# Adding half of the expert outputs on the chip instead of in DRAM, in a two-block layer on one core

## The chip, the cores and the metric

The kernel runs on one core of one Trainium2 chip. The metric is the device time of one execution in microseconds; lower is better. Times of runs are given as a median with the lowest and the highest.

## The reference, cut to what matters

Two transformer blocks run one after the other on 512 tokens of width 1024, in float32. Only the end of the second block matters here: a mixture of 32 experts in four groups, of which every token takes two.

```python
def hierarchical_moe(h, w_rg, b_rg, w_re, b_re, w_gate, w_up, w_down):
    ...
    out = jnp.zeros_like(tok)
    for e in range(N_EXPERTS):
        hid = jax.nn.silu(tok @ w_gate[e]) * (tok @ w_up[e])
        out = out + combine[:, e:e + 1] * (hid @ w_down[e])
    return out.reshape(b, s, d)
...
        x = x + gate_f * hierarchical_moe(h, ...)
    return rmsnorm(x, norm_final)
```

`w_gate[e]` and `w_up[e]` are 1024 x 256, `w_down[e]` is 256 x 1024; one expert has 3 MB of weights. `combine` is zero but for the two experts of each token.

## The kernel before, in words

Everything ahead of the experts (first block, mixer, router) is not touched. Then 17 *units* follow (`units`, line 1176): 16 pairs of experts and one unit "x" of 64 slots for the tokens that did not fit into a pair. A pair has 128 slots, 64 for each expert; a slot holds a token's number (`slot_t`, `slot_i`) and its weight (`slot_w`). In the loop's order the units have the places 0 to 16, "x" is place 4.

For a unit the loop at line 1771 does this:

- `load_piece` (line 1183) loads the expert weights in pieces of 1 MB, in SP's queue, into a ring of places in SBUF (`ring`, line 1607): a piece goes where the piece 17 places earlier was. The halves of a unit's gate and up weights come first, then its down weights.
- `gather` (line 1581, POOL's queue, an indirect DMA) fetches the 128 tokens of the unit two places later from `hs` in DRAM.
- `gate_up` (line 1634) is 16 matmuls in float32 (32 in the profile, since each float32 matmul has two entries there), two experts side by side on 64 columns each; ScalarE and VectorE make `hid`.
- `front` (line 1614) transposes the gathered tokens of the next unit into `xe`.
- `hid_T` (line 1646) transposes `hid` into `hT_`.
- `down` (line 1654) multiplies by the down weights, 8 matmuls (16 entries) into two banks; VectorE scales both halves into `y`.
- `scatter_add` (line 1589, POOL's queue, an indirect DMA with addition) adds the rows of `y` to the tokens' rows in `yd`, a tensor in DRAM that holds the residual stream.

The last unit (place 16) is not added in DRAM. In the loop's `else` the 512 rows of `yd` are read back into `xtok` in four DMAs of 512 KB on SP's queue (line 1797), which wait for all 16 additions, and `combine` (line 1675) adds the last unit on the chip: `down` builds a one-hot table `oh` of 128 x 512 (slot against token), a matmul with `oh` as the stationary operand brings the slots' rows to their tokens, and VectorE adds the bank to `xtok`. Eight blocks (four token tiles, two column halves) make one call. `finish_half` then normalises and stores.

`down` and `combine` know two forms already: with `yl` given, `y` is split into a rounded part `yh` and a rest `yl`, both in the rounded format F32R, and both are multiplied; without it `y` stays float32. The form with two parts was used only in the loop behind the end for tokens beyond "x", which does not run here.

The order on each engine is planned when the program is built: instructions that are ready in the planner's model may come ahead of earlier ones of the program text; each engine then runs its list in order. A small set of tile names is shared: `whi` and `wlo` (three buffers each) hold weight pieces as well as the tiles `parts_y` and `ylast` take.

Of the kernel before, what the change touches and what calls it, by code (L numbers as in the profile page):

```python
# [19 lines left out]
F32 = mybir.dt.float32  # L20
F32R = mybir.dt.float32r
# [24 lines left out]
def tile_kernel(ctx: ExitStack, tc: tile.TileContext, A, out, dbg=None, stop=None):  # L46
    nc = tc.nc
# [11 lines left out]
    def mm(ps, l, r, start, stop):  # L59
        nc.tensor.matmul(ps, l, r, start=start, stop=stop, skip_group_check=True)  # L60

    def bk():
        return ps_mm.tile([128, 512], F32, name="mm")
# [171 lines left out]
    with tc.tile_pool(name="b1x", bufs=1, reuse_waits="tile") as b1x:  # L235
# [14 lines left out]
        for k in range(8):  # L250
# [10 lines left out]
            if k >= 3 and k < 7:  # L261
                i = k - 3
# [285 lines left out]
    with tc.tile_pool(name="mgs", bufs=1, reuse_waits="tile") as mgs, \  # L548
            tc.tile_pool(name="mg", bufs=1, reuse_waits="tile") as mg:
        mrg = (mg.tile([128, 8, 512], F32R, name="mrh"), mg.tile([128, 8, 512], F32R, name="mrl"))  # L550
        for m in range(8):
            sg = []
            for i in range(2):
                c0 = 3072 + i * 1024 + m * 128
                ps = dense(wload(w_in[:, c0:c0 + 128], 8, 128), u)
                t = mgs.tile([128, 512], F32, name="sg", bufs=6)
# [150 lines left out]
    with ExitStack() as mls:  # L707
# [25 lines left out]
        for hf in range(2):  # L733
            hid = (ml.tile([128, 16, 512], F32R, name="hidh"), ml.tile([128, 16, 512], F32R, name="hidl"))
            for m in range(16):
                c0 = hf * 2048 + m * 128
                ps = dense(wload(A["w_mlp_in"][0][:, c0:c0 + 128], 8, 128), u)
                t = ml.tile([128, 512], F32, name="rl", bufs=3)
# [5 lines left out]
            for m in range(8 - hf):  # L744
# [5 lines left out]
                t = ml.tile([128, 512], F32, name="mo", bufs=2)  # L750
# [12 lines left out]
        t = ml.tile([128, 512], F32, name="mo", bufs=2)  # L763
# [41 lines left out]
    for ts in halves:  # L805
        for k in range(8):
            t = n2.tile([128, 256], F32, name="hmt", bufs=6)
# [349 lines left out]
    xtok = me.tile([128, 4, 1024], F32, name="xtok")  # L1157
# [18 lines left out]
    units = list(range(XU)) + ["x"] + list(range(XU, NP))  # L1176
# [6 lines left out]
    def load_piece(n, place, e=None, eng=None, cols=False):  # L1183

        u, a, i = todo[n]
        pick = lambda w: w[NP * i + u] if e is None else w[bass.ds(e, 1)].rearrange("a k n -> (a k) n")
        if cols:
            for j, t in enumerate(place):
                nc.sync.dma_start(t.rearrange("p (k n) -> p k n", k=2),
                                  pick(wd_)[:, j * 512:(j + 1) * 512].rearrange("(p k) n -> p k n", p=128))  # L1190
            places[n] = None, place
            return


        ws = (pick(wd_),) if a == 2 else (pick(wg_), pick(wu_))
        kb = (2 if a == 2 else 4) // len(place)
        for j, t in enumerate(place):
            k0 = (0 if a == 2 else 4 * a) + j * kb
            for g, w in enumerate(ws):
                (eng or nc.sync).dma_start(t.rearrange("p (g k n) -> p g k n", k=kb, g=len(ws))[:, g],  # L1200
                                           w.rearrange("(p k) n -> p k n", p=128)[:, k0:k0 + kb, :])
        places[n] = place

    def weights(u):

        def block(ns, k, w):
            kb = 2048 // w
            place = places[ns[k // kb]]
            if place[0] is None:
                return [t[:, k * 512:(k + 1) * 512] for t in place[1]]  # L1210
            k, kb = k % kb, kb // len(place)
            if w == 512:
                return place[k // kb].rearrange("p (g k n) -> p k g n", g=2, k=kb)[:, k % kb]
            b = place[k // kb][:, k % kb * w:(k % kb + 1) * w]
            return [b[:, :512], b[:, 512:]]
        ns = [[todo.index((u, a, i)) for a in range(3)] for i in ((0,) if u == "x" else (0, 1))]
        return [(lambda k, n=n: block(n[:2], k, 512), lambda k, n=n: block(n[2:], k, 1024)) for n in ns]
# [135 lines left out]
    yd = dr.tile([512, 1024], F32, name="yd")  # L1353
# [227 lines left out]
    def gather(idx):  # L1581
        x = wp.tile([128, 1024], F32, name="raw", bufs=NRAW)
        n = idx.shape[0]
        gathers.append(nc.gpsimd.indirect_dma_start(out=x[:n], out_offset=None, in_=hs,
                                     in_offset=bass.IndirectOffsetOnAxis(ap=idx, axis=0),
                                     bounds_check=511, oob_is_err=False))
        return x
# [9 lines left out]
    mw = ctx.enter_context(tc.tile_pool(name="mw", bufs=1, side="right", reuse_waits="tile"))  # L1597
# [36 lines left out]
    def gate_up(xe, ws, n):  # L1634

        pg = ps_s.tile([128, 512], F32, name="sc")
        for k in range(8):
            for h, w in enumerate(ws):
                pq = slice(64 * h, 64 * h + 64)
                mm(pg[pq].rearrange("p (g n) -> p g n", g=2), xe[:, k, pq], w[0](k), k == 0, k == 7)  # L1640
        hid = mw.tile([128, 256], F32, name="hid")
        silu[0] = nc.scalar.activation(hid[:n], pg[:n, :256], AF.Silu)  # L1642
        nc.vector.tensor_mul(hid[:n], hid[:n], pg[:n, 256:])
        return hid
# [9 lines left out]
    def down(hT_, ws, n, tokf, wsl, yh, yl=None):  # L1654

        oh = None
        if tokf is not None:
            oh = mw.tile([128, 512], F32R if yl is not None else F32, name="oh", bufs=1)
            nc.vector.tensor_scalar(oh[:n], io512[:n], tokf, None, op0=OP.is_equal)
        for j in range(2):  # L1660
            c = slice(j * 512, (j + 1) * 512)
            py = bk()
            for k in range(2):
                for h, w in enumerate(ws):
                    pq = slice(64 * h, 64 * h + 64)
                    mm(py[pq], hT_[:, k, pq], w[1](k)[j], k == 0, k == 1)
            y = yh[:, c] if yl is None else sqacc
            nc.vector.scalar_tensor_tensor(y[:n], py[:n], wsl, gfb[:n, c], op0=OP.mult, op1=OP.mult)
            if yl is None:
                continue  # L1670
            nc.scalar.activation(yh[:n, c], y[:n], AF.Copy)
            nc.vector.tensor_sub(yl[:n, c], y[:n], yh[:n, c].bitcast(F32))
        return n, oh, yh, yl

    def combine(parts, done=None):

        for i, j in [(m % 4, m // 4) if done is None else (m // 2, m % 2) for m in range(8)]:
            c = slice(j * 512, (j + 1) * 512)
            ps = bk()
            ms = [(oh[:n, i * 128:(i + 1) * 128], y[:n, c]) for n, oh, *ys in parts for y in ys if y is not None]  # L1680
            for k, (t, y) in enumerate(ms):
                mm(ps, t, y, k == 0, k == len(ms) - 1)
            nc.vector.tensor_add(xtok[:, i, c], xtok[:, i, c], ps)
            if done:
                done(i, j)
# [68 lines left out]
    def over_slots():  # L1754

        lp = ps_t.tile([64, NX], F32, name="tp")
        for n in range(8):
            mm(lp, POt[:, n, :], CT[:, n, 0, :], n == 0, n == 7)
        lw = ps_t.tile([64, 3, NX], F32, name="tp")
        for n in range(8):  # L1760
            mm(lw, POw[:, n, :], CW[:, n], n == 0, n == 7)
        ls = rt.tile([64, 2, NX], F32, name="ls")
        nc.vector.tensor_scalar(ls[:, 0], lp, 512.0, None, op0=OP.add)
        nc.vector.tensor_reduce(ls[:, 1], lw.rearrange("p m c -> p c m"), axis=AX.X, op=OP.add)
        nc.sync.dma_start(ltd, ls.rearrange("p a c -> p (a c)"))
        nc.vector.tensor_copy(xslot, ls[:, :, 0])
        nc.vector.tensor_copy(xslot_i, ls[:, 0, 0:1])

    parts_y = lambda: (wp.tile([128, 1024], F32R, name="whi", bufs=NHI), wp.tile([128, 1024], F32R, name="wlo", bufs=NLO))
    ylast = lambda: wp.tile([128, 1024], F32, name="whi", bufs=NHI)  # L1770
    for t, u in enumerate(units):
        n, tokf, wsl, idx = slot(u)
        e = nc.sync.value_load(eid[0:1, 0:1], min_val=0, max_val=NE - 1) if u == "x" else None
        for m, key in enumerate(todo):
            if key[0] == u and m not in places:
                place = ring[m - 2]
                if m == len(todo) - 1 and len(place) == 1:

                    place = [place[0][:, :1024], place[0][:, 1024:]]
                load_piece(m, place, e, cols=m == len(todo) - 1)  # L1780
        ws = weights(u)
        if t + 2 < len(units):
            xs_[units[t + 2]] = gather(slot(units[t + 2])[3])
        hid = gate_up(xe_[u], ws, n)
        if t == 0:
            over_slots()
        if t + 1 < len(units):
            v = units[t + 1]
            xe_[v] = front(xs_[v], slot(v)[0])
        hT_ = hid_T(hid, n)  # L1790
        if t + 1 < len(units):
            y = mw.tile([128, 1024], F32, name="y", bufs=2)
            down(hT_, ws, n, None, wsl, y)
            scatter_add(idx, y[:n])
        else:
            for i in range(4):
                nc.sync.dma_start(xtok[:, i, :], yd[i * 128:(i + 1) * 128, :])
            parts = [down(hT_, ws, n, tokf, wsl, ylast())]


    nf = wp.tile([128, 1024], F32, name="raw", bufs=NRAW)
# [24 lines left out]
    with tc.For_i(0, more, 1) as it:  # L1826
# [11 lines left out]
        ws = weights("x")  # L1838
# [37 lines left out]
```

## Time and profile before

| | before |
|---|---|
| median of 3 runs | 1392.52 us (1388.49 to 1395.84) |
| profiled execution, its own time | 1396.43 us |
| span of that execution | 1394.6 us |
| granted TensorE clock, mean share | 0.971 |
| busy share of the span: PE, DVE, ACT, POOL | 92%, 50%, 33%, 14% |
| stage of the experts | about 1090 to 1370 us |

PE is TensorE's matmuls, DVE VectorE, ACT ScalarE, POOL GpSimd, SP the engine whose queue loads the weights. The span lies inside the run's own time. Durations of matmuls overlap in the records; their pitch is read from start to start. In the rows, "idle before" is the time that the engine stood still in front of an instruction, and the name behind the arrow is what ended it. `L60` is the helper that records nearly all matmuls; they are told apart by their tiles: `sc` is gate-up, `mm<-...,hT_` the down matmuls, `mm<-...,oh` the additions by one-hot table, `tp<-ident,raw` and `po` the transposes. The number behind `hT__` names the unit: 9490 is place 0, 9909 place 6, 10135 place 9, 10634 place 16.

### The profile page before, as it was taken

Reading aid. Unit: us, or ns where it says so; the run is one execution under the profiler, and the core shown is the slowest. Engines: PE = TensorE matmul, PEld = TensorE weight load, DVE = VectorE, ACT = ScalarE, POOL = GpSimd, SP = SyncE. Lnnn points to the kernel's source line nnn. Section 1 sums busy time; section 2 is a strip of 40 time slices with the busy share of each in tenths; the row PEclk is TensorE's granted clock in tenths of the full one; section 3 lists DMA queues with packets and bytes.
Section 4 is the critical chain, followed back from the end, with each engine's and each line's share of the span. In section 5 each row is a group of like instructions: output and inputs, shape, how many; then the busy total and the mean of one; then the engine's idle time right before and its main releaser. Section 6 shows DMA issues by size and latency. Waiting matters only on the chain.

```text
span 1394.6 us, 20149 instructions
## 1 busy us (share of the span) xinstructions
PE 1287.2 (92%) x8021; PEld 946.3 (68%) x8021; DVE 700.8 (50%) x1187; ACT 458.7 (33%) x803; POOL 194.4 (14%) x227
## 2 busy tenths in 40 slices
PE   7999999999989999999999989999999599877874
PEld 6797778888878788887888876986667244322321
DVE  6546677534477764347457543256674522212214
ACT  4343343423444322334235514424535111101103
POOL 2000002000312200132112000001031121211101
PEclk9899999999999999999999999999999699999998
DMA  7222225335357754336341522231775799999994
GB/s 220 73 80 70 76 58 162 117 91 156 91 181 255 234 178 145 95 96 207 93 134 53 152 58 69 85 84 54 256 263 181 268 386 356 367 365 319 400 363 152
DMA packets 202351, 245.56 MB, mean 176 GB/s; under 512 B 11733, under 2 KB 161199, under 8 KB 198416
## 3 DMA queue, kind: packets, MB, share of 16 engines
q1 hardware_dynamic: 194848, 226.49, 49.0%
q0 software_dynamic: 7392, 17.76, 4.4%
q8 instruction: 64, 1.05, 0.3%
q14 instruction: 31, 0.25, 0.1%
q10 hardware_dynamic: 16, 0.00, 0.0%
HBM read 232.15 MB, written 19.19 MB: 180 GB/s over the span
## 4 chain that ended last, share of the span: by engine, by line
PE 68%; DMA 18%; DVE 7%; issue 3%; ACT 3%; SPq 0%; POOL 0%; DVEq 0%; ACTq 0%; POOLq 0%
PE mm L60 53%; PE sc L60 10%; DMA adw<-in_w_ada_dram 3%; PE po L60 3%; DMA ON<-in_expert_w_up_dram 2%; DMA pc<-in_expert_w_up_dram 2%; PE tp L60 1%; DMA pc<-in_expert_w_gate_dram 1%; DVE adacc L609 1%; DVE wlo L115 1%; DMA ON<-in_expert_w_down_dram 1%; DMA ON<-in_expert_w_gate_dram 1%; DMA pc<-in_expert_w_down_dram 1%; DMA mh<-in_expert_w_down_dram 1%; DMA mh<-in_expert_w_up_dram 1%
## 5 line engine op out<-in xcount | busy, mean ns | idle before, releaser
L114 ACT ACTIVATE whi<-raw 128x1024 fp32r<-128x1024 f32 (+1 forms) x157 | 163.4, 1043 | 367.7 <-PE mm L60 276.6
L115 DVE TENSOR_TENSOR wlo<-raw,whi 128x1024 fp32r<-128x1024 f32 (+1 forms) x157 | 195.6, 1248 | 173.1 <-ACT whi L114 172.9
L60 PE MATMUL mm<-uh,whi 128*128 128x512 f32 x528 | 210.6, 399 | 2.9 <-ACT uh L154 1.5
L60 PE MATMUL mm<-ul,whi 128*128 128x512 f32 x528 | 209.9, 398 | 0.5 <-DVE ul L155 0.5
L60 PE MATMUL mm<-uh,wlo 128*128 128x512 f32 x528 | 209.5, 397 | 0.0
L60 PE MATMUL sc<-pc,xe 128*64 128x512 f32 x296 | 106.5, 623 | 14.0 <-DMA pc<-in_expert_w_up_dram 13.7
L60 PEld LDWEIGHTS mm<-uh,whi 128*128 128x128 f32 x528 | 100.8, 191 | 26.2 <-ACT uh L154 2.3
L60 PEld LDWEIGHTS mm<-ul,whi 128*128 128x128 f32 x528 | 100.8, 191 | 23.6 <-issue 1.7
L60 PEld LDWEIGHTS mm<-uh,wlo 128*128 128x128 f32 x528 | 101.0, 191 | 22.2 <-issue 1.0
L60 PE MATMUL mm<-hidh,whi 128*128 128x512 f32 (+1 forms) x272 | 103.9, 382 | 0.0
L60 PE MATMUL mm<-hidh,wlo 128*128 128x512 f32 (+1 forms) x272 | 103.2, 379 | 0.0
L60 PE MATMUL mm<-hidl,whi 128*128 128x512 f32 (+1 forms) x272 | 102.0, 375 | 0.0
L740 POOL TENSOR_TENSOR rl<-rl 128x512 f32<-128x512 f32 x32 | 50.2, 1568 | 228.6 <-ACT rl L739 228.6
L1642 ACT ACTIVATE hid<-sc 128x256 f32<-128x256 f32 (+1 forms) x17 | 6.5, 383 | 210.6 <-PE sc L60 210.6
L60 PEld LDWEIGHTS sc<-pc,xe 128*64 128x64 f32 x296 | 33.1, 143 | 58.6 <-issue 55.2
L609 DVE SCALAR_TENSOR_TENSOR adacc<-adw,cact,adacc 128x1024 f32<-128x1024 f32 x42 | 56.9, 1356 | 25.5 <-DMA adw<-in_w_ada_dram 24.8
L60 PE MATMUL mm<-mh,whi 128*128 128x512 f32 (+1 forms) x168 | 67.9, 404 | 0.0
L60 PE MATMUL mm<-mh,wlo 128*128 128x512 f32 (+1 forms) x168 | 66.8, 398 | 0.0
L60 PE MATMUL mm<-mlo,whi 128*128 128x512 f32 (+1 forms) x168 | 66.2, 394 | 0.0
L1628 DVE TENSOR_SCALAR xe<-tp,sge 128x128 f32<-128x128 f32 (+1 forms) x68 | 24.2, 400 | 80.7 <-PE sc L60 65.1
L60 PEld LDWEIGHTS mm<-hidh,wlo 128*128 128x128 f32 x272 | 51.0, 188 | 10.6
L60 PEld LDWEIGHTS mm<-hidl,whi 128*128 128x128 f32 x272 | 51.1, 188 | 10.4 <-issue 0.2
(622 smaller groups left out, 2374.2 us busy)
## 6 DMA issues: line engine op xcount, KB each, us to landing
raw<-in_w_in_dram SPq DMA_DIRECT2D x68, 512.0 KB
adw<-in_w_ada_dram SPq DMA_DIRECT2D x24, 1024.0 KB
pc<-in_expert_w_gate_dram SPq DMA_DIRECT2D x37, 512.0 KB
pc<-in_expert_w_up_dram SPq DMA_DIRECT2D x37, 512.0 KB
raw<-in_w_mlp_in_dram SPq DMA_DIRECT2D x32, 512.0 KB
raw<-in_w_mlp_out_dram SPq DMA_DIRECT2D x32, 512.0 KB
pc<-in_expert_w_down_dram SPq DMA_DIRECT2D x16, 1024.0 KB
ON<-in_expert_w_down_dram SPq DMA_DIRECT2D x5, 1024.0 KB
```

Source lines behind the costliest of these rows:

```text
L60: nc.tensor.matmul(ps, l, r, start=start, stop=stop, skip_group_check=True)
L114: nc.scalar.activation(hi, raw, AF.Copy)
L115: nc.vector.tensor_sub(lo, raw, hi.bitcast(F32))
L609: nc.vector.scalar_tensor_tensor(acc[s], w[:, k, :], c, acc[s], op0=OP.mult, op1=OP.add)
L740: nc.gpsimd.tensor_mul(t, t, t)
L1628: nc.vector.tensor_scalar(xe[:, f, :], tp[:, k * n:(k + 1) * n], sge[:, 1, f:f + 1], sge[:, 0, f:f + 1], op0=OP.mult, op1=OP.add)
L1642: silu[0] = nc.scalar.activation(hid[:n], pg[:n, :256], AF.Silu)
```

## The change

Places 0 to 7 are still added in DRAM. At place 8 the tokens' rows are read back, now on POOL's queue, and from there on every unit's output is kept on the chip in the form with two parts; each time two units are there, the next pass of the loop adds them to `xtok` by one call of `combine` with both (four matmuls for a block instead of one). The last unit alone is added behind the loop as before, in float32. Two sets of buffers alternate: one from `whi` and `wlo`, one in the tiles that the DRAM additions used (`yh`, `yl`, in place of the two buffers of `y`). `oh` has two buffers.

```diff
--- before.py
+++ after.py
@@ -1655,7 +1655,7 @@
         oh = None
         if tokf is not None:
-            oh = mw.tile([128, 512], F32R if yl is not None else F32, name="oh", bufs=1)
+            oh = mw.tile([128, 512], F32R if yl is not None else F32, name="oh", bufs=2)
             nc.vector.tensor_scalar(oh[:n], io512[:n], tokf, None, op0=OP.is_equal)
@@ -1768,6 +1768,9 @@
     ylast = lambda: wp.tile([128, 1024], F32, name="whi", bufs=NHI)
+
+    AWAY = 8
+    ybuf, parts = [], []
     for t, u in enumerate(units):
@@ -1788,14 +1791,19 @@
         hT_ = hid_T(hid, n)
-        if t + 1 < len(units):
-            y = mw.tile([128, 1024], F32, name="y", bufs=2)
+        if t < AWAY:
+            y = mw.tile([128, 1024], F32, name="yl" if t % 2 else "yh")
             down(hT_, ws, n, None, wsl, y)
             scatter_add(idx, y[:n])
-        else:
+            continue
+        if t == AWAY:
             for i in range(4):
-                nc.sync.dma_start(xtok[:, i, :], yd[i * 128:(i + 1) * 128, :])
-            parts = [down(hT_, ws, n, tokf, wsl, ylast())]
+                nc.gpsimd.dma_start(xtok[:, i, :], yd[i * 128:(i + 1) * 128, :])
+            ybuf += [parts_y(), (mw.tile([128, 1024], F32R, name="yh"), mw.tile([128, 1024], F32R, name="yl"))]
+        if len(parts) == 2:
+            combine(parts)
+            parts = []
+        parts.append(down(hT_, ws, n, tokf, wsl, *(ybuf[t % 2] if t + 1 < len(units) else [ylast()])))
```

## Rows read from the trace of the kernel before

**Rows 1.** Busy time by stretch: us, PE, PEld, DVE, ACT, POOL, clock, DMA, GB/s.

```profile
1175.70:1187.90 12.20, 12.20 (x61) 6.40 (x60) 3.54 (x8) 1.89 (x5) 2.61 (x2) 1.00 1.03 370
1224.00:1361.00 137.00, 105.73 (x413) 37.96 (x413) 24.70 (x53) 11.05 (x31) 17.39 (x13) 0.95 0.98 363
```

**Rows 2.** PE's timeline: the first down matmul of place 0 and of place 6.

```profile
1114.64 0.60 PE L60 MATMUL mm<-pc,hT__9490 128*64 128x512 f32 x2
...
1187.22 0.64 PE L60 MATMUL mm<-pc,hT__9909 128*64 128x512 f32 x1
```

**Rows 3.** PE's timeline, places 9 to 16: matmuls that waited for weights.

```profile
1239.68 3.22 PE L60 MATMUL mm<-pc,hT__10135 128*64 128x512 f32 x11 [1.37 <-DMA pc<-in_expert_w_down_dram]
...
1242.73 0.59 PE L60 MATMUL mm<-pc,hT__10135 128*64 128x512 f32 x1
...
1253.03 1.51 PE L60 MATMUL sc<-pc,xe 128*64 128x512 f32 x6 [3.23 <-DMA pc<-in_expert_w_up_dram]
...
1269.17 0.64 PE L60 MATMUL sc<-mlo,xe 128*64 128x512 f32 x1 [1.34 <-DMA mlo<-in_expert_w_up_dram]
...
1290.55 1.09 PE L60 MATMUL sc<-pc,xe 128*64 128x512 f32 x1 [4.11 <-DMA pc<-in_expert_w_up_dram]
...
1325.56 0.61 PE L60 MATMUL sc<-mh,xe 128*64 128x512 f32 x1 [1.98 <-DMA mh<-in_expert_w_up_dram]
...
1343.78 5.30 PE L60 MATMUL sc<-pc,xe 128*64 128x512 f32 x14 [2.49 <-DMA pc<-in_expert_w_up_dram]
...
1360.87 0.61 PE L60 MATMUL sc<-ON,xe 128*64 128x512 f32 x1 [1.46 <-DMA ON<-in_expert_w_up_dram]
```

**Rows 4.** The chain that ended last, its end: start, us, what.

```profile
1336.28 14.23 DMA pc<-in_expert_w_down_dram
...
1350.57 10.16 DMA ON<-in_expert_w_up_dram
...
1360.87 3.63 PE sc L60 x14
...
1366.44 7.87 PE mm L60 x24
```

**Rows 5.** POOL's timeline: additions in DRAM (`yd<-y`) and one gather.

```profile
1211.01 1.58 POOL L1590 DMA_INDIRECT yd<-y,slot_i  x1 [11.80 <-DVE y L1668]
...
1224.33 1.61 POOL L1590 DMA_INDIRECT yd<-y,slot_i  x1 [4.43 <-DVE y L1668]
1226.24 1.03 POOL L1584 DMA_INDIRECT raw<-hs,slot_i  x1 [0.30 <-issue]
...
1355.80 1.56 POOL L1590 DMA_INDIRECT yd<-y,slot_i  x1 [16.62 <-DVE y L1668]
```

**Rows 6.** DMA queue (packets, MB, share of 16 engines), 1350 to 1360 us.

```profile
q1 hardware_dynamic: 1094, 4.11, 102.4%
```

**Rows 7.** DMA queues, 1320 to 1330 us: weights, and one addition.

```profile
q1 hardware_dynamic: 929, 3.45, 85.4%
q0 software_dynamic: 144, 0.31, 15.7%
```

**Rows 8.** DMA queues, 1338 to 1348 us: weights, and one addition.

```profile
q1 hardware_dynamic: 644, 3.38, 87.9%
q0 software_dynamic: 144, 0.25, 13.1%
```

**Rows 9.** SP's queue: its wait (us in total, times, longest), and the issues.

```profile
SPq L1797 <- DMA yd<-y,slot_i: 10.0, 1, 10.0
...
1365.70 1.77 SPq L1797 DMA_DIRECT2D xtok<-yd  x4
```

**Rows 10.** VectorE: groups and first addition; the one-hot table; TensorE's last part.

```profile
L1683 DVE TENSOR_TENSOR xtok<-xtok,mm 128x512 f32<-128x512 f32 x8 | 5.4, 681 | 0.6 <-PE mm L60 0.5
...
1371.71 0.69 DVE L1683 TENSOR_TENSOR xtok<-xtok,mm 128x512 f32<-128x512 f32 x1 [0.30 <-PE mm L60]
...
L1659 DVE TENSOR_SCALAR oh<-rbc,slot_t x1: 481/481/481, 1090.3 to 1090.3; 128x512 f32<-128x512 f32 x1
...
1370.54 7.19 PE L60 MATMUL mm<-whi,oh 128*128 128x512 f32 x16
```

**Rows 11.** POOL's timeline: another plain load of 512 KB.

```profile
1303.91 0.60 POOL L1802 DMA_DIRECT2D raw<-in_norm_final_dram  x1 [18.71 <-PE tp L1621]
```

**Rows 12.** PE's timeline in a dense stage: first and last of 54 matmuls.

```profile
699.69 0.39 PE L60 MATMUL mm<-hidh,wlo 128*128 128x512 f32 x1
...
711.82 0.39 PE L60 MATMUL mm<-hidl,whi 128*128 128x512 f32 x1
```

**Rows 13.** ScalarE, groups of the whole span: a rounding of 128 x 512.

```profile
L154 ACT ACTIVATE mrh<-t 128x512 fp32r<-128x512 f32 x8 | 5.0, 630 | 19.8 <-POOL t L569 19.8
```

## The prediction

> **What bounds the kernel now.** I read the page's slices first, then the stage of the experts alone, and in it the engines in order: TensorE's timeline, its waits, the DMA queues by stretch, the chain that ended last. Places 0 to 16 are the 17 units in the loop's order; the place with the extra experts is 4.
>
> Two regimes follow each other. In places 0 to 6 TensorE never stops (12.20 us busy of 12.20) and the weights loaded ahead are used up; from 1224 to 1361 it is busy for 105.7 of 137.0 us while the 16 DMA engines are busy for 98% [rows 1]. In the first regime six places take 1187.22 - 1114.64 = 72.6 us, so a place costs TensorE **12.1 us** when nothing is late [rows 2]. In the second, almost every place stops for its weights: the places 9, 10, 11, 12, 14, 15 and 16 each have a matmul that waited for a landing [rows 3]. The chain that ended last says the same: DMA 14.2 us, DMA 10.2 us, then place 16's gate-up, its down matmuls, and the additions [rows 4]. The last weights that count land at 1360.87; place 16's down matmuls end at 1370.54, 9.7 us later [rows 3, 10], and the output is stored by 1394.6. So what the change is worth is decided by when place 16 ends; the 24.1 us behind that are the same work in both kernels.
>
> **What it removes.** Eight additions in DRAM, of places 8 to 15, the first issued at 1224.33 and the last at 1355.80 [rows 5]. Their POOL time (1.6 us each) lies on an engine with nothing else to do. Their DMA time does not: in the ten microseconds with no addition in flight the weights' queue moved 4.11 MB [rows 6]; in two stretches with one addition in each it moved 3.45 and 3.38 MB, although the addition itself is only 0.31 and 0.25 MB [rows 7, 8]. The queue's total hardly differs, so one addition displaces 0.66 to 0.73 MB of weights, at 0.411 MB/us **1.6 to 1.8 us**. A lower bound is its bytes alone, 0.25 / 0.411 = 0.6 us. I take 1.6, since two stretches show it. The seven of places 8 to 14 have landed before 1360.9: 7 x 1.6 = 11.2 us of landing time.
>
> It also takes four read-backs out of SP's queue at the end. SP waits there 10.0 us for the last addition to land and issues them at 1365.70 [rows 9]. Behind them on SP are only the output's stores, which wait for later work, and the first addition to the tokens on VectorE started at 1371.71, 0.3 us after idling for TensorE and not for the rows [rows 10]. That removal is worth nothing by itself, but it would have become the limit had place 16 ended some microseconds sooner.
>
> **What it moves.** The same 2.1 MB are read back at place 8, by POOL. The price is 2.1 / 0.411 = **5.1 us** of landing time for whatever is in flight [rows 6], between about 1221 and 1231. Four issues at 0.60 us (the row of another plain load on POOL) are 2.4 us of POOL [rows 11]. They must wait until place 7's addition, issued at 1211.01, has landed, some 10 us later (the last addition, issued at 1355.80, was waited for until 1365.70 [rows 5, 9]). Behind them on POOL stands the gather of place 11, at 1226.24 [rows 5]; it is needed some 25 us later, so the wait is covered. If that cover went, place 11's transposes would be late.
>
> **What it adds.** Four pairs are added on the chip inside the loop, at places 10, 12, 14 and 16: each 8 blocks x 4 matmuls of 512 columns in the rounded float format. Their duration reads 0.39 us, but they overlap: in the dense stage 54 such matmuls start between 699.69 and 711.82, one every 12.13 / 53 = 0.229 us [rows 12]. So a pair costs TensorE 32 x 0.229 = **7.3 us**, four 29.3 us. An upper bound is the full duration, 0.39 x 32 = 12.5 us. I take 0.229: same shape, type and engine, each with its own weight load. The last unit alone stays as it is.
>
> VectorE gets 32 adds of 0.68 us, 16 subtractions at about that price and eight one-hot tables of 0.48 us, some 37 us [rows 10]; ScalarE 16 roundings at 0.63 us, 10 us [rows 13]. VectorE is busy for 24.7 of these 137 us and ScalarE for 11.1 [rows 1]. A block's add (0.68) is shorter than its four matmuls (0.92) and three banks rotate, so TensorE doesn't wait. The halves of one unit share one scratch tile, a serial chain of some 4 us (two adds or subtractions and a rounding, twice) behind the down matmuls; nothing needs it before the pair is added, over a place later. All this costs nothing as long as VectorE stays under half busy.
>
> The Trainium skill's page "DMA: Bandwidth & Descriptors", in "Anatomy of one DMA — SWDGE (gpsimd) path", gives a DMA of this queue a fixed 2 us, mostly waiting for the write's receipt, and movement by bytes / 436 GB/s; by that an addition of 0.25 MB takes 0.57 us of the engines, and the eight removed give back less than the read-back costs. Rows 7 and 8 speak against it for additions; by the page the sum would come out on the slow side, which is rival 2 below.
>
> **The sum.** A place whose second half of gate-up starts at landing L ends at L + 9.7 if its additions are out of the way; otherwise it ends 12.1 (with a pair 19.4) after the place before. Landings shift by +5.1 for the read-back and -1.6 for each addition that is gone.
> - Place 9 waited for 1239.68 and ended at 1243.3 [rows 3]; now +5.1 - 1.6: 1246.8.
> - 10: landing 1253.0 + 5.1 - 3.2 = 1254.9, so 1264.6; by TensorE 1246.8 + 19.4 = 1266.2. 11: landing 1269.5, 1279.2; by TensorE 1278.3.
> - 12: TensorE 1279.2 + 19.4 = 1298.6, landing 1289.3 + 9.7 = 1299.0. 13: 1311.1. 14: 1330.5 (landing 1321.1, not a limit).
> - 15: landing 1343.8 + 5.1 - 11.2 = 1337.7, so 1347.4. 16: TensorE 1347.4 + 19.4 = 1366.8; landing 1360.9 - 6.1 = 1354.8, 1364.5, or **1371.8** if the pair is added wholly behind that landing.
>
> Place 16 so ends between 1366.8 and 1371.8 against 1370.5: -3.7 to +1.3 us. The program's order is planned ahead: the one-hot table written at the end of the loop was computed at 1090.3 [rows 10], so additions that are ready probably fill the waits; but the planner's waits are not the chip's. I take -2. Against the profiled execution's own 1396.43 us that is 1394.4; the runs' median is 3.9 us lower, so 1392.52 - 2 = **1390.5**. What the DMA queues get back, TensorE's additions take.
>
> **The rivals.**
> 1. *All of the additions fall into waits.* TensorE then runs without a stop from place 9: 1246.8 + 7 x 12.1 + 29.3 = 1360.8, 9.7 us sooner: about 1383. For it: 31 us idle of 137 [rows 1], as much as the additions need. Against it: places 11, 12 and 15 still hang on landings in the sum; these would have to come some 4 us earlier again, as they would if an addition's uneven load on the engines costs more than the 1.6 us.
> 2. *The last pair stands behind the last weights, and the DMA gives nothing back.* The place is 16: with 0.6 us for each addition, seven give 4.3 us and the read-back takes 5.1, so the landing comes at 1361.7; half a gate-up and the transposes, then 7.3 us of additions before the down matmuls: 1361.7 + 9.7 + 7.3 - 0.5 = 1378.2, +7.7: about 1400. It decides as soon as an addition gives back under 0.75 us and the planner puts the pair behind the gate-up. Against it rows 7 and 8; for it that units and additions stand in that order in the program.
> 3. *The matmuls cost their duration.* 128 x 0.39 = 50 us, 20 us more than above, with TensorE the bound: about 1411. Rows 12 speak plainly against it.
>
> That the change doesn't do what it says has no case: no wait remains that could keep the eight in DRAM.
>
> **The numbers.** Forecast 0.57, its own range 1386 to 1398; rival 1 0.22, rival 2 0.16, rival 3 0.05. Range 1382.5 to 1400: it reaches to rivals 1 and 2 and leaves out rival 3 and what lies beyond them. 0.5% (7.0 us) is about what a measurement here can tell from no change. Faster by more is rival 1, 0.22; slower by more rivals 2 and 3, 0.21; within it 0.57.
>
> **What would show it.** Right: 128 matmuls of the one-hot tiles at 0.23 us from start to start; TensorE at over 90% from 1250 to 1366 and its waits for weights there down from 31 us to under 10; 1.6 us fewer landing time for each addition gone and a dip at the read-back near 1225; place 16's landing near 1355, with some additions between it and the down matmuls. Wrong: SP waiting for TensorE to free places, a gather late behind the read-back, VectorE in front of TensorE's additions, or a landing of place 16 at or after 1361.

## The result, and the profile after

The changed kernel takes **1406.2 us** (median of 7; 1399.3 to 1408.6) against 1394.7 us for the kernel before in the same comparison (median of 7; 1388.5 to 1396.8). The ratio is 1.0084, with a 95% interval of 1.0057 to 1.0111: slower, by 8 to 15 us. The forecast was 1390.5 us, 2 us under the 1392.5 us that the kernel before took in its first three runs, and the range ended at 1400. The profiled execution of after has a span of 1405.1 us and its own time is 1406.78 us.

**TensorE is the bound now.** The first row below is the window of 1224 to 1361 us (columns as in [rows 1]), where TensorE was busy for 105.7 us before. The other three are TensorE's waits there (in total, times, longest).

```profile
1224.00:1361.00 137.00, 127.00 (x519) 52.93 (x520) 54.61 (x101) 22.07 (x49) 7.56 (x10) 1.00 0.95 376
```

```profile
PE po L1649 <- DVE hid L1643: 4.1, 4, 1.1
PE sc L60 <- DMA whi<-in_expert_w_up_dram: 1.8, 1, 1.8
...
PE sc L60 <- DMA wlo<-in_expert_w_up_dram: 1.3, 1, 1.3
```

Of seven places that stood for weights [rows 3] two short waits are left, 3.1 us together. The weights do come sooner. SP issues its last two loads only once loads ahead of them have landed: of the time that SP waited from 1180 to 1350 us in after, 123.8 us ended with a landing and 3.4 us with TensorE. So this issue dates the whole stream. In after it is at 1344.33; in before it was at 1353.13 (both rows below). Place 0's first down matmul, against which I align the executions, stands at 1116.49 in after and at 1114.64 in before [rows 2]; so the stream is 8.8 + 1.85 = 10.65 us earlier in these two executions. The read-back that was paid for this stands on POOL at place 8, 8 us behind the last addition in DRAM (by the program it has to wait for that landing; the profile calls the wait `issue`), and shares the engines with the weights, which move 1.81 MB in ten microseconds instead of 4.11 [rows 6] (first POOL's timeline in after, then SP's in before and in after, then the queues of after from 1220 to 1230 us: packets, MB, share):

```profile
1215.46 1.59 POOL L1590 DMA_INDIRECT yd<-yl,slot_i  x1 [13.24 <-DVE yl L1668]
...
1223.61 2.21 POOL L1801 DMA_DIRECT2D xtok<-yd  x4 [3.82 <-issue]
```

```profile
1353.13 1.80 SPq L1189 DMA_DIRECT2D pc<-in_expert_w_down_dram  x2
...
1344.33 1.80 SPq L1189 DMA_DIRECT2D pc<-in_expert_w_down_dram  x2
```

```profile
q1 hardware_dynamic: 712, 1.81, 48.9%
q0 software_dynamic: 533, 1.46, 43.2%
```

**And yet place 16 is later.** Its down matmuls start at 1377.29 (before 1366.44 [rows 4]) and the final additions at 1380.88 (before 1370.54 [rows 10]): 10.3 us, of which 1.85 were there at place 0, before any unit is added on the chip. What lies behind is as long as before (1405.1 - 1380.9 = 24.2 us). Here is the chain that ended last, from place 14's down matmuls on (start, us, what):

```profile
1340.03 3.65 PE mm L60 x16
1343.68 6.92 PE sc L60 x32
...
1352.54 7.29 PE mm L60 x22
1359.83 1.00 PE sc L60 x2
1360.84 2.53 PE mm L60 x10
1363.37 3.58 PE sc L60 x14
1366.94 0.90 PE mm L60 x3
1367.85 1.00 PE sc L60 x2
1368.85 2.51 PE mm L60 x10
1371.36 3.58 PE sc L60 x14
...
1377.29 7.37 PE mm L60 x24
```

A gate-up is 32 entries `sc`. Place 15's run through in 6.92 us. Place 16's are cut by three groups of additions (`mm`) into 2 + 14 + 2 + 14 and take 1.00 + 3.58 + 1.00 + 3.58 = 9.16 us: **2.2 us more for the same work**. TensorE's timeline shows why:

```profile
1352.54 1.93 PE L60 MATMUL mm<-pc,hT__10748 128*64 128x512 f32 x4 [0.52 <-DVE hT__10748 L1651]
1354.40 0.50 PE L60 MATMUL mm<-whi,oh 128*128 128x512 f32 x1
1354.83 3.65 PE L60 MATMUL mm<-pc,hT__10748 128*64 128x512 f32 x12
1358.41 0.50 PE L60 MATMUL mm<-wlo,oh 128*128 128x512 f32 x1
...
1372.19 0.59 PE L60 MATMUL sc<-ON,xe 128*64 128x512 f32 x1
1372.20 0.59 PE L60 MATMUL sc<-pc,xe 128*64 128x512 f32 x1
1372.62 0.59 PE L60 MATMUL sc<-ON,xe 128*64 128x512 f32 x1
1372.63 0.59 PE L60 MATMUL sc<-pc,xe 128*64 128x512 f32 x1
```

The last four rows are the undisturbed form: the matmuls of the two experts, 64 columns each (`128*64`), start 10 ns apart and the next two 0.43 us later; they share the array. An addition is 128 columns wide. Put between the two halves it leaves one of them alone: two entries of one expert take 1.00 us there, while in company four entries, two of each expert, take 0.86. In the first four rows one single addition parts place 15's down matmuls: place 14's 16 entries take 3.65 us in the chain; here the next work after the 16 entries starts at 1358.41, 5.87 us after the first. The four entries ahead of the addition take 1.86 us, one after the other, where four entries in company take 0.86. One addition, 0.23 us in a row of its kind, costs about **2.2 us** here, and each of the two cuts in place 16's gate-up, where two entries were left alone, about 1.1 us.

The Trainium skill's page "TensorE: Matmul & The Clock Gate", in "Part 3: Packing small matmuls — row/col tiling", has matmuls on different tiles of the array run at the same time, and all matmuls start and end in program order. The first agrees with the 10 ns above. From the second it follows that a full-width matmul which stands between two halves in the program's order keeps the later half from starting beside the earlier one, and the rows agree: the parted entries run alone. The change of width as such costs little: where the additions end and half-width matmuls begin in e1_block (the first experiment below), 0.31 us lie between the starts, 0.08 more than between two additions.

```profile
1362.58 0.39 PE L60 MATMUL mm<-yl,oh 128*128 128x512 f32 x1
1362.89 0.64 PE L60 MATMUL mm<-ON,hT__10802 128*64 128x512 f32 x1
```

### The profile page after: what moved, and what is told of

It is laid out like the page before. It is cut to its first block, busy times and chain, and to the rows that moved or that the text cites. A ratio compares the mean times of both kernels' runs of the same rounds, so it can differ in the third digit from the quotient of the medians.

```text
span 1405.1 us, 20458 instructions
## 1 busy us (share of the span) xinstructions
PE 1317.5 (94%) x8149; PEld 963.9 (69%) x8149; DVE 736.8 (52%) x1243; ACT 469.0 (33%) x819; POOL 183.5 (13%) x223
## 4 chain that ended last, share of the span: by engine, by line
PE 71%; DMA 14%; DVE 8%; ACT 3%; issue 3%; SPq 0%; POOL 0%; DVEq 0%; ACTq 0%; POOLq 0%
PE mm L60 55%; PE sc L60 10%; DMA pc<-in_expert_w_up_dram 3%; PE po L60 3%; DMA adw<-in_w_ada_dram 2%; PE tp L60 2%; DMA pc<-in_expert_w_gate_dram 1%; DVE wlo L115 1%; DMA whi<-in_expert_w_gate_dram 1%; DVE adacc L609 1%; DMA whi<-in_expert_w_up_dram 1%; DMA wlo<-in_expert_w_up_dram 1%; DMA pc<-in_expert_w_down_dram 1%; DMA raw<-hs,slot_i 1%; DMA raw<-in_w_in_dram 1%
## 5 line engine op out<-in xcount | busy, mean ns | idle before, releaser
L60 PEld LDWEIGHTS sc<-pc,xe 128*64 128x64 f32 x296 | 30.0, 137 | 42.7 <-issue 40.0
L60 PEld LDWEIGHTS mm<-hidh,whi 128*128 128x128 f32 x272 | 51.1, 188 | 9.3 <-issue 0.2
```

## The experiments

All kernels ran against the kernel before. *Stage* is from place 0's first down matmul to the first matmul of the final additions in the profiled execution; it was 255.9 us before (1370.54 - 1114.64) and is 264.4 after (1380.88 - 1116.49). The executions differ by up to 7 us in when place 0 comes, so the stage tells more of a part than a single span does. It is read from one execution of each kernel; e1_block and e4_block_ohlate, with the same order on TensorE, differ by 2.5 us in it.

| kernel | us | before | ratio, 95% interval | stage |
|---|---|---|---|---|
| the change | 1406.2 | 1394.7 | 1.0084, 1.0057 to 1.0111 | 264.4 |
| e1_block | 1392.2 | 1394.0 | 0.9985, 0.9964 to 1.0005 | 252.4 |
| e2_ohlate | 1400.4 | 1394.0 | 1.0067, 1.0036 to 1.0097 | 263.7 |
| e3_noadd | 1385.1 | 1394.0 | 0.9937, 0.9914 to 0.9960 | 244.5 |
| e6_traffic | 1407.5 | 1394.0 | 1.0092, 1.0060 to 1.0123 | 268.4 |
| e4_block_ohlate | 1392.0 | 1392.7 | 0.9996, 0.9979 to 1.0014 | 254.9 |
| e7_block_away9 | 1396.1 | 1392.7 | 1.0021, 1.0003 to 1.0039 | 257.0 + 3.7 |
| e8_block_away7 | 1392.1 | 1392.7 | 0.9994, 0.9976 to 1.0012 | 249.3 + 3.7 |
| e9_block_nolast | 1382.6 | 1392.7 | 0.9939, 0.9917 to 0.9961 | 246.0 |
| e10_split | 1389.6 | 1392.9 | 0.9982, 0.9961 to 1.0003 | 254.4 |
| e11_split_away7 | 1391.4 | 1392.9 | 0.9985, 0.9967 to 1.0002 | 254.2 + 3.7 |
| e12_split7_readback | 1391.4 | 1392.4 | 0.9982, 0.9962 to 1.0002 | 249.1 + 3.7 |
| e13_block7_readback | 1391.4 | 1392.4 | 0.9994, 0.9973 to 1.0015 | 251.6 + 3.7 |

"+ 3.7" marks kernels whose final additions take in one more unit: from the first final addition to the end of the span they take 27.8 to 27.9 us, e1_block 24.1.

### 1. The same additions, but in one block

```diff
-        hid = gate_up(xe_[u], ws, n)
+        with tc.issue_after(added[0].ins) if added[0] else ExitStack():
+            hid = gate_up(xe_[u], ws, n)
...
         if len(parts) == 2:
-            combine(parts)
+            with tc.issue_after(hidt[0].ins):
+                combine(parts)
             parts = []
-        parts.append(down(hT_, ws, n, tokf, wsl, *(ybuf[t % 2] if t + 1 < len(units) else [ylast()])))
+        with tc.issue_after(added[0].ins) if added[0] else ExitStack():
+            parts.append(down(hT_, ws, n, tokf, wsl, *(ybuf[t % 2] if t + 1 < len(units) else [ylast()])))
```

`issue_after` keeps what stands inside it behind the named instruction in the planned order: the 32 additions stand behind the transposes of `hid`, and no gate-up or down matmul ahead of them.

> The changed kernel, but TensorE's 32 matmuls of a pair are queued in one piece: behind the transposes of hid, and ahead of the unit's down matmuls and of the next unit's gate-up. Same work, same DMA. Theory A (TensorE is the bound, and the additions are planned in small groups between the experts' matmuls, which then no longer run two side by side: in the changed kernel a half gate-up of place 16 takes 1.00 + 3.58 us instead of 3.5, the down matmuls of place 15 1.93 + 3.65 instead of 3.6): 4 to 5 us for a pair of places come back, 15 to 18 in all, so about 1390 us, level with the kernel before or a few us under it. Rival B (VectorE's order holds TensorE up: one-hot table and an addition to the tokens ahead of hid): within 4 us of the changed kernel's 1406. Rival C (it is the work itself, 32 matmuls and 8 adds a pair): 1406.

Measured 1392.2 us: 14.0 us less than the change (15 to 18 were expected), by the order alone; 12.0 us of it show in the stage of the two profiled executions. The chain of this kernel, and its row of the same window (1224 to 1361):

```profile
1323.79 10.95 PE mm L60 x48
1334.73 6.92 PE sc L60 x32
...
1343.59 3.71 PE mm L60 x16
1347.29 6.88 PE sc L60 x32
...
1355.60 14.66 PE mm L60 x56
```

```profile
1224.00:1361.00 137.00, 122.90 (x545) 57.48 (x542) 58.29 (x105) 22.41 (x48) 4.34 (x5) 0.99 0.93 367
```

32 additions and 16 entries of a down make 10.95 us together, so the 32 cost 10.95 - 3.6 = 7.3 us, and every gate-up runs in 6.9. TensorE does more matmuls in the window than after (545 against 519) in 4.1 us less busy time, and in the whole stage the same 1037 entries keep it busy for 232.8 us instead of 247.1. From place 12's first down matmul to place 14's it takes 1331.08 - 1298.03 = 33.1 us, and from there to place 16's 31.8; in the change 1340.03 - 1302.36 = 37.7 and 37.3. So these two pairs alone lose 10.1 of the 12.0 us by which the stages differ (264.4 - 252.4). Against the kernel before, what is left is no difference that can be measured.

### 2. The one-hot table later on VectorE

VectorE's timeline of after shows another suspect: in front of place 16 the table `oh` stands ahead of `hid`, and an addition ahead of the copy to `hT_`.

```profile
1375.40 0.49 DVE L1659 TENSOR_SCALAR oh<-rbc,slot_t 128x512 f32<-128x512 f32 x1 [3.56 <-PE mm L60]
1375.81 0.41 DVE L1643 TENSOR_TENSOR hid<-hid,sc 128x256 f32<-128x256 f32 x1
1376.14 0.68 DVE L1683 TENSOR_TENSOR xtok<-xtok,mm 128x512 f32<-128x512 f32 x1
1376.81 0.42 DVE L1651 COPY hT__10802<-po 128x256 f32<-128x256 f32 x1
```

```diff
-            nc.vector.tensor_scalar(oh[:n], io512[:n], tokf, None, op0=OP.is_equal)
+            with tc.issue_after(copied[0].ins) if copied[0] else ExitStack():
+                nc.vector.tensor_scalar(oh[:n], io512[:n], tokf, None, op0=OP.is_equal)
```

> The changed kernel, but every one-hot table is queued on VectorE behind the copy of hT of its own unit, so that it can no longer stand in front of hid and of that copy. Theory A: 0 to 4 us sooner than the changed kernel, 1402 to 1406. Rival B: the end of an even place's gate-up to its down matmuls shrinks from some 3.4 to 2.4 us and more, 1396 or less. Rival C: 1406.

> The first experiment, and the one-hot table is computed behind the copy of the transposed hidden values. If VectorE's order costs time of its own beside TensorE's order, 1 to 2 us under the first experiment (1390.5 to 1391.5); if the 6 us that the late table alone gave in the second experiment came from shorter interleaving on TensorE, nothing is left to gain and it stays within 1 us of 1392.2.

Alone (e2_ohlate) the edit gave 1400.4 us, between what theory A and rival B had named. Its interval overlaps that of the change, and its stage is shorter by 0.7 us only: of the 7.4 us between the two profiled executions 6.7 lie ahead of place 0 (1109.80 against 1116.49), which the edit doesn't touch. So the 6 us between the medians are not shown to come from VectorE's order. On top of the block (e4_block_ohlate) it gave 1392.0 against 1392.2 us: no gain. A microsecond or two can't be told from chance here. What VectorE's additions cost in front of `hid` was not tried apart from TensorE's order; but the busy time that e1_block takes off TensorE (247.1 to 232.8 us) is more than the whole difference of the stages, which leaves nothing for VectorE to explain.

### 3. No additions, and all of the traffic

Two kernels take the two sides of the change apart. e3_noadd leaves the outputs of places 8 to 15 out of the result: their tables and scaled outputs are made, but not added. e6_traffic adds on the chip as the change does and sends the same eight units to DRAM as well, after the read-back.

```diff
# e3_noadd
         if len(parts) == 2:
-            combine(parts)
             parts = []
# e6_traffic
         parts.append(down(hT_, ws, n, tokf, wsl, *(ybuf[t % 2] if t + 1 < len(units) else [ylast()])))
+        if t + 1 < len(units):
+            scatter_add(idx, parts[-1][2][:n].bitcast(F32))
```

> The changed kernel without the four additions of pairs inside the loop: the outputs of places 8 to 15 are computed and split, and then left out of the result. The DMA side of the change alone. Theory A and rival C: TensorE is idle again and place 16 hangs on its landing, which comes 8 to 12 us sooner than before: about 1382 to 1386 us. Rival D (the read-back in the middle costs as much landing time as the eight additions in DRAM gave): 1392 or more.

> The changed kernel, and in addition the eight additions in DRAM of places 8 to 15 are issued as before (the rounded part, to rows that nobody reads any more). The TensorE side of the change alone, with the DMA traffic of before put back. Theory A and rival C: TensorE is the bound from place 10 on and hides most of it: 1406 to 1410 us. Rival D: the landings matter, each addition 1.6 us: 1417 or more.

Without the additions the time is 1385.1 us, 9 us under before, the stage 11.4 us shorter: this is what the DMA side gives while nothing is added on the chip. TensorE stands for weights again, as in this row (place 12):

```profile
1287.22 1.09 PE L60 MATMUL sc<-pc,xe 128*64 128x512 f32 x1 [3.62 <-DMA pc<-in_expert_w_up_dram]
```

With all of the traffic the time is 1407.5 us, 1.3 above the change, no difference that can be measured (its stage is 4.0 us longer): TensorE's longer work hides most of some 16 us of DMA. SP's last issue in e6_traffic gives the prices:

```profile
1356.80 1.81 SPq L1189 DMA_DIRECT2D pc<-in_expert_w_down_dram  x2
```

Behind place 0's first down matmul (1113.02 there) that is 243.8 us; it is 238.5 before and 227.8 after. Before and e6_traffic have seven additions in DRAM ahead of this issue and differ by the read-back: **5.3 us**. After has none of the seven: 16.0 us, **2.3 us for each addition**. These are differences between single executions. The seven kernels with after's DMA work have the date at 227.2 to 230.5 (e1_block and e4_block_ohlate), though TensorE's work differs, so an addition comes to 1.9 to 2.4 us and the read-back to about 5. It is a mean over seven, and what it takes of the engines' own time is not shown: from 1280 to 1285 in e6_traffic the DMA engines are busy for only 67%, so a part of the delay is time in which the stream stood still. It does not hold for one addition more or fewer: e7_block_away9 below has one more ahead of this issue and the date at 236.0, and the four kernels with seven additions in all have it at 228.4 to 230.7, no earlier than after.

### 4. Where the last pair stands, and how many there are

In e1_block the pair of units 14 and 15 stands in front of place 16's down matmuls with nothing to hide it. e9_block_nolast is e1_block without that pair: units 14 and 15 are left out of the result. e7_block_away9 and e8_block_away7 change `AWAY = 8` to 9 and 7: pairs are added at odd places, and unit 15 goes into the final additions.

> The first experiment without the last pair: units 14 and 15 are left out of the result, their tables and scaled outputs are still made. If the last pair stands wholly exposed in front of place 16's down matmuls, the time falls by 7.3 us from 1392.2 to about 1385, and place 16's down starts right behind its transposes. If the weights of place 16 are the limit there, it falls by less than 4 us (1388.5 or more).

> The order of the first experiment (a unit's 32 additions in one block, placed behind the transposes of the next unit but one), and nine units added in DRAM instead of eight: pairs are added at places 11, 13 and 15, and unit 15 goes with the last unit into the call behind the loop. If what is left over the kernel before in that order is the last pair in front of place 16's down matmuls (32 matmuls, 7.3 us at a pitch of 0.229), then this kernel has nothing there and pays 16 more matmuls of two parts at the end, 3.7 us: 3 to 4 us under the first experiment's 1392.2, about 1388.5, and 4 to 5 us under the kernel before. If the ninth addition in DRAM (2 us of landing) makes place 16's weights the limit again, it gains less than 2 us on the first experiment.

> The same order, seven units added in DRAM: pairs at 9, 11, 13 and 15, and unit 15 goes into the call behind the loop. One addition in DRAM fewer than the first experiment (2 us of landing), the same number of pairs in the loop, none of them in front of place 16. If landings still limit some of the places 11 to 15 it comes out at or below the kernel with nine (1387 to 1389); if TensorE is the bound from place 9 on, the fourth pair costs its 7.3 us less what falls into waits, and it lies 2 to 6 us above the one with nine (1390 to 1394).

The last pair was exposed: 1382.6 us without it, 9.6 under e1_block (7.3 expected; the stage is 6.5 us shorter), and place 16's down starts right behind the copy:

```profile
1352.27 0.64 PE L60 MATMUL mm<-ON,hT__10802 128*64 128x512 f32 x1 [0.52 <-DVE hT__10802 L1651]
```

The other three cost almost nothing: with no pair (e3_noadd) the stage is 244.5 us, with three (e9_block_nolast) 246.0, with four (e1_block) 252.4, where each pair takes TensorE 7.3 us. The three fall into time in which TensorE would otherwise stand for the weights of a later place; behind the last pair no weights are left to wait for.

But moving the last pair did not pay. e7_block_away9 was expected at 1388.5 and took 1396.1 us. TensorE stood 17.0 us for landings in its stage, against 10.9 in e1_block; it still did so at place 13, where e1_block's last such wait was at place 10 (1251.77). The first row below (place 10) shows a second cost. While TensorE stood for 4.1 us the granted clock fell to 0.50, the lower of its two levels (1.2 GHz of 2.4); it came back about 5 us after the work had begun again, and 16 entries took 6.26 us instead of 3.65:

```profile
1248.13 6.26 PE L60 MATMUL sc<-pc,xe 128*64 128x512 f32 x16 [4.13 <-DMA pc<-in_expert_w_up_dram]
...
1306.76 3.65 PE L60 MATMUL sc<-pc,xe 128*64 128x512 f32 x14 [1.03 <-DMA pc<-in_expert_w_up_dram]
```

So an addition is cheap only where TensorE would wait for weights without it. How the loss of e7_block_away9 divides between the ninth addition in DRAM, the clock and the places of its pairs stays open: no run changes one of these alone. With seven in DRAM (e8_block_away7, 1392.1 us) TensorE waits 0.2 us for weights in all from 1224 on; it can't gain more there. Its expectation named both outcomes, 1387 to 1389 and 1390 to 1394; the second came. The extra unit in the final additions costs 3.7 us. The rows of e7_block_away9 show most of it: a block of two rounded and two float32 entries starts every 1.32 us, a block of two float32 entries every 0.9 (16 in 7.2 us), over eight blocks 3.4 us.

```profile
1369.11 0.79 PE L60 MATMUL mm<-yh,oh 128*128 128x512 f32 x1
1369.74 0.39 PE L60 MATMUL mm<-yl,oh 128*128 128x512 f32 x1
1369.97 1.02 PE L60 MATMUL mm<-whi,oh 128*128 128x512 f32 x2
1370.43 0.80 PE L60 MATMUL mm<-yh,oh 128*128 128x512 f32 x1
```

### 5. Looking for a version that beats both

In e1_block TensorE stands still for 1.0 us in each of six places, between gate-up and the transposes of `hid`. e10_split puts half of a pair there, at a point where no couple of matmuls is parted; e11_split_away7 is the same with seven units in DRAM. The edit against e1_block, cut to what matters:

```diff
+        if len(parts) == 2:
+            with tc.issue_after(gate[0].ins):
+                combine(parts, ms=range(4))
+        with tc.issue_after(added[0].ins) if added[0] else ExitStack():
-        hT_ = hid_T(hid, n)
+            hT_ = hid_T(hid, n)
...
-                combine(parts)
+                combine(parts, ms=range(4, 8))
```

> The first experiment with each pair's 32 additions cut into two blocks of 16: one right behind the gate-up matmuls, where TensorE otherwise stands still for 1.0 us until hid is there, and one behind the transposes of hid, where it fills the 0.5 us until they are copied. No group of the experts' half-width matmuls is broken. TensorE is the bound from place 11 on, so each pair behind that point (12, 14, 16) should cost 1.0 us less: 3 us under the first experiment, about 1389. If the handover to VectorE, which then has its additions in front of hid and of the copy, gives that back, it stays at 1392 or above.

> The same cut into two blocks with seven units added in DRAM, pairs at 9, 11, 13 and 15. TensorE waited 6.0 us for hid there and 0.2 us for weights. Four times 1.0 us less than the uncut order with seven (1392.1): about 1388. If VectorE's additions in front of hid cost as much as the hole that they fill, 1392.

The holes were filled: these are the waits of e10_split from 1224 to 1375, where e1_block has 6.0 us in six.

```profile
PE po L1649 <- DVE hid L1643: 3.1, 3, 1.0
```

The time is 1389.6 us, close to the 1389 expected, but the stage is 254.4 us against 252.4, so the 2.6 us between the medians are not shown to come from the edit. In the stage TensorE's waits for VectorE fell from 8.2 to 4.3 us, but the same 1037 entries kept it busy for 236.7 us instead of 232.8, at a mean granted clock of 0.97 instead of 0.99 (0.57 from 1230 to 1235, mostly the lower level, behind waits of 0.9 and 2.9 us for weights). e11_split_away7 stayed at 1391.4. In its profiled execution TensorE stood for a gather that POOL had issued behind the read-back. e12_split7_readback and e13_block7_readback issue the read-back behind that gather (`if t == AWAY + 1`, with `issue_after` the gather):

> Seven units added in DRAM, pairs cut into two blocks, and the read-back issued behind the gather of place 10 instead of ahead of it. In the run before this one TensorE stood 9.4 us for that gather, whose rows are transposed ahead of place 8's down matmuls. If that wait was time of the whole, this kernel takes 5 to 9 us less than that one's 1391.4: 1382 to 1387, under both kernels of the case. If the weights that land later in its place take it up, it stays within 2 us of 1391.

> The same with each pair's additions in one block. There the wait for the gather was 2.75 us in the profiled execution: 1 to 3 us under 1392.1, about 1390, and 3 us over the cut order if filling the 1.0 us holes in front of hid pays.

```profile
1224.20 1.94 PE L1621 MATMUL tp<-ident,raw 128*128 128x128 f32 x8 [9.40 <-DMA raw<-hs,slot_i]
```

```profile
1202.88 1.94 PE L60 MATMUL sc<-ON,xe 128*64 128x512 f32 x2 [5.17 <-DMA ON<-in_expert_w_up_dram]
...
1216.44 0.61 PE L60 MATMUL sc<-mh,xe 128*64 128x512 f32 x1 [1.76 <-DMA mh<-in_expert_w_up_dram]
```

The first row is e11_split_away7, the others e12_split7_readback. The wait for the gather is gone and the stage is 5 us shorter, but the median is the same 1391.4. The profiled execution of e11_split_away7 took 1395.06 us, 3.6 over its median, so the 9.4 us were probably not in every execution. The two waits for weights are no price of the later read-back: e8_block_away7, which reads back early, has them too (4.85 and 1.65 us). Neither hoped-for gain came. **No version is measurably faster than the kernel before**; the best four lie 1 to 3 us under it with intervals that cross 1.

## Why the prediction was wrong, point by point

- *The step that failed is TensorE's side of the sum*: "TensorE 1279.2 + 19.4", a place at 12.1 us plus a pair at 7.3 us. Both prices hold when each runs through: the pitch of 0.229 us, 7.3 us for 32 and 6.9 for a gate-up are all in e1_block. They don't add when the planner weaves the one into the other: a matmul of an addition between the halves of a couple leaves each half to run alone, 1.1 to 2.2 us a cut. Two places with a pair were to take 2 x 12.1 + 7.3 = 31.5 us; the change takes 37.7 and 37.3, and e1_block 33.1 and 31.8.
- A later sentence, "additions that are ready probably fill the waits; but the planner's waits are not the chip's", had the cause within reach: I read the planner's freedom as a gain that might fail to come, and gave it no price of its own. The forecast's end of place 16, 1366.8 to 1371.8, became 1380.9 (1379.0 with place 0 aligned). The block alone gives 1366.5 (1367.1 aligned).
- *The read-back* was right: 5.1 us forecast, 5.3 between two executions. Its wait on POOL cost nothing at place 8, as forecast; in e8_block_away7 and e11_split_away7, where it comes a place sooner, the gather behind it was late (2.75 and 9.4 us) in the way that the text named.
- *An addition in DRAM* was sized too low: 1.6 us forecast, 2.3 measured as a mean over seven (1.9 to 2.4). I had left the larger bound (1.8) for the range; rows 7 and 8 probably catch only a part of what an addition displaces. So the stream of weights gained 10.65 us, not 6.1, and this error of the sum lay on the other side: alone it would have made the kernel faster. From the rate in the Trainium skill's page "DMA: Bandwidth & Descriptors", section "Anatomy of one DMA — SWDGE (gpsimd) path", bytes over 436 GB/s, 0.57 us is the estimate for its 0.25 MB. The measured delay of the stream is about four times that, and it decides, for additions.
- *The shift of the bound* was right and went further than the sum: TensorE waits for weights 3.1 us in the window (under 10 forecast) and is busy for 93% of it. The "31 us" that the prediction set against this is all of TensorE's idle time from 1224 to 1361 before; 21.3 us of it were waits for weights.
- *VectorE and ScalarE at nothing* was not contradicted: VectorE is busy for 40% of the window, and e2_ohlate and e4_block_ohlate show no gain from its order that can be told from chance.
- *Rival 1* (additions all in waits, 1383) had the landings right, 4 us sooner than the sum as it demanded; interleaving took more than it gave. *Rival 2*, at 1400, was wrong in its cause: the seven additions give back 16.0 us, three times the read-back, and place 16 does not stand for its weights. Its other half, a last pair that nothing hides, is what e9_block_nolast shows for the block order. *Rival 3*, at 1411 the nearest number (4.8 us off), charged all 128 matmuls their duration; in the block they start every 0.23 us, and the 12 us are paid by the experts' matmuls, not by the additions.

## What to carry to other kernels

Matmuls that share the array side by side are one block of work: whatever else is ready must go between blocks, and an order that a planner makes from its own waits has to be held to that (here 12 us of a 264 us stage, for the same matmuls). Work moved from DMA to TensorE is free only in the stretch where TensorE waits for DMA; price it at the end of the stretch, not by the idle time of the whole. A pitch read where a kind of matmul runs alone is a lower bound, until a row shows the mixture.

## What the runs showed of the hardware that I had not expected

A single full-width matmul put among half-width ones that run side by side cost about 2.2 us where it left four entries alone (5.87 instead of 3.65), nearly ten times its own pitch of 0.229, and about 1.1 us where a cut left two alone. An indirect addition in DRAM of 0.25 MB delayed the weights' stream by 2.3 us as a mean over seven, nearly four times its bytes at the stream's rate of 0.411 MB/us (0.6 us); single additions more or fewer did not follow this mean. And behind a TensorE at 93% some 16 us of additional DMA work were nearly free: e6_traffic is 1.3 us over the change, its stage 4.0 us.
